# A residual kept in SBUF ahead of sliding window attention, and the sink's logit as a column of its scores

## The chip, the cores and the metric

The kernel runs on one core of a Trainium2 chip. A core has five engines that run side by side, each through its own list of instructions in order: TensorE (PE, matrix products), VectorE (DVE), ScalarE (ACT), GpSimd (POOL) and SyncE (SP), which here only issues DMA transfers. They wait for each other by semaphores. The metric is the time of one execution on the device in microseconds; several executions are taken, and their median is given.

## What is computed

Two transformer blocks follow each other on 1024 tokens with 1024 channels. The first has differential attention, stick-breaking attention, cross attention and an MLP, and ends in an RMS norm whose result is the second block's input `x`. The second block norms `x`, projects it by `w_in`, and runs three mixers: sliding window attention (8 heads, 2 key heads, window 128, with a sink per head), RWKV7 and a gated linear attention (GLA). Their outputs are joined, projected by `w_out`, normed and added to `x`. Two places matter here:

```python
# sliding window attention: a sink's logit is one more column of the softmax, and is dropped
s = jnp.where(valid[None, :, None, None], s, -jnp.inf)
sink = jnp.broadcast_to(sinks..., s.shape[:-1] + (1,))
p = jax.nn.softmax(jnp.concatenate([s, sink], axis=-1), axis=-1)[..., :-1]
o = jnp.einsum('bnhgqk,bnkhd->bnqhgd', p, vb)
...
# end of the second block
y = jnp.concatenate([attn, rwkv, gla], axis=-1) @ w_out
return x + gate[:, None] * _rmsnorm(y, g_post)
```

## The kernel before, in words

Activations lie with channels on the 128 partitions and tokens along the free axis. The 1024 tokens are worked in two halves of 512, the "first half" and the "second half". Products in 32 bits are made of three matmuls (lines 208 to 210) of a high and a low part; a weight tile is split into the two by ScalarE (line 200, `L200`) and then VectorE or GpSimd (`L201`). Streams between stages go through memory: `hd` is the first block's stream ahead of its last norm, `pd` the projections, `yd` the mixers' outputs, `zd` the first half's product with `w_out`, `out` the result.

The order of each engine's instructions is set by a scheduler that replays the program as it is written; what is written is itself an interleaving. `weave(main, fill, ratio)` takes steps of `main` and puts in between steps of `fill` of a cost in the given ratio; both are Python generators. In the part at hand there are two weaves:

- the first half's window attention (`g_window0`) with projections of the second half (`g_p2a`, `g_p2b`), at 0.9;
- as `main`, the second half's recurrences (`g_rec(1)`) and then its window attention (`g_tail`, that is `g_window(1)`); as `fill` (named `rest`), what is left of the projections, then `g_wout2` and `g_wout2a`, the product of the first half's mixers with `w_out`, at 0.28. Beside `g_wout2a` runs `g_final0`, the first half's last norm and sum. What of `rest` is left is used up inside `finish`, the second half's product with `w_out`, norm and sum.

`win_load` loads queries and keys of a half through three staging tiles named `ws` with the tag `wp`, and splits them (`stack_k`, `stack_q`; lines 441, 442, 454 to 457). `w_units` makes eight units of it, one per block of 128 queries and key head, each for four query heads, in three steps. Step `a`: scores (L1667, L1668) into PSUM; VectorE scales them, adds the mask's bias and writes them to `p` (L1670, twice per unit, two heads each) and takes the maximum (L1671, twice); then the sink: maximum with the sink's logit (L1673), sink less maximum (L1674), minus the maximum (L1675), its exponential on ScalarE (L1676). ScalarE takes the exponential of the four heads with their sums (L1678), VectorE adds the sink's share (L1681) and takes the reciprocal (L1682), ScalarE scales two heads (L1684) and GpSimd two (L1685). Step `tr`: transposes on TensorE (L1699), copied to SBUF by ScalarE (L1702). Step `pv`: product with the values (L1709), times the gate on VectorE (L1711), and for the second half a split into `yw`. `p` has the tag `wp` too, three buffers for the staging tiles and for the units' scores.

`g_final0` works through eight rows of 128 channels: it loads a row `h` of `hd` and a row `z` of `zd` (tiles `t` with the tag `t2`, five buffers, which others use too), makes `h` times gain and norm (L2314) and `z` times gate, gain and norm (L2316) on VectorE, adds them on GpSimd (L2317) and stores the row to `out`. `finish` loads weights (`wload`, L2332), splits them into `wb` and `wh`, loads the second half's residual `fh`, and multiplies `yw` with `wb` and `wh`.

## Time and profile of the kernel before

| what | us |
|---|---|
| median of 3 runs (2345.37 to 2354.68) | 2347.19 |
| the profiled execution | 2346.06 |
| its span, from its first instruction to its last | 2344.3 |
| TensorE busy in it (share of the span) | 2245.4 (96%) |
| VectorE busy | 1292.4 (55%) |
| ScalarE busy | 1034.7 (44%) |
| GpSimd busy | 691.2 (29%) |

The profile is a recording of one execution. It has a page with shares of each engine, and views of the trace behind it: a table by stretches of the span, the instructions of an engine in order of time with the idle time before each and what ended it (the timeline), groups of instructions by line and operation, what an engine waited for (the waits), and the chain of work that ended last, followed back from the last instruction. `L1675` is line 1675 of the kernel. Times of instructions are in microseconds from the span's start.

The first half's units run from about 1930 to 2005 us, the second half's from 2228 to 2300. The finish's first matmul starts at 2299.40 us, and the span ends 45 us later.

### The profile page before, as it was taken

Reading aid. Unit: us, or ns where it says so; the run is one execution under the profiler, and the core shown is the slowest. Engines: PE = TensorE matmul, PEld = TensorE weight load, DVE = VectorE, ACT = ScalarE, POOL = GpSimd, SP = SyncE. Lnnn points to the kernel's source line nnn. Section 1 sums busy time; section 2 is a strip of 40 time slices with the busy share of each in tenths; the row PEclk is TensorE's granted clock in tenths of the full one; section 3 lists DMA queues with packets and bytes.
Section 4 is the critical chain, followed back from the end, with each engine's and each line's share of the span. In section 5 each row is a group of like instructions: output and inputs, shape, how many; then the busy total and the mean of one; then the engine's idle time right before and its main releaser. Section 6 shows DMA issues by size and latency. Waiting matters only on the chain.

```text
span 2344.3 us, 34760 instructions
## 1 busy us (share of the span) xinstructions
PE 2245.4 (96%) x13056; PEld 1898.0 (81%) x13056; DVE 1292.4 (55%) x2312; ACT 1034.7 (44%) x2196; POOL 691.2 (29%) x1035
## 2 busy tenths in 40 slices
PE   8999999999999999999999999999999999989886
PEld 7898999988898888888888888887787776677765
DVE  7665656676754554422423422346846658656485
ACT  6655656674643424411311311344633348434463
POOL 4101100000500003556565650035322333224343
PEclk9999999999999999999999999999998999989898
DMA  4010010123241211222222221133343233533461
GB/s 135 28 42 23 31 39 28 46 77 124 66 140 54 99 37 45 75 79 72 77 83 72 78 74 45 52 124 122 119 134 105 74 127 100 166 126 105 131 208 50
DMA packets 116393, 200.06 MB, mean 85 GB/s; under 512 B 14048, under 2 KB 33792, under 8 KB 115456
## 3 DMA queue, kind: packets, MB, share of 16 engines
q1 hardware_dynamic: 111456, 184.72, 24.1%
q0 software_dynamic: 4768, 13.11, 1.7%
q8 instruction: 102, 1.67, 0.3%
q14 instruction: 67, 0.55, 0.1%
HBM read 163.70 MB, written 34.08 MB: 84 GB/s over the span
## 4 chain that ended last, share of the span: by engine, by line
PE 56%; DVE 8%; DMA 4%; ACT 2%; issue 2%; POOL 1%; SPq 0%; DVEq 0%; ACTq 0%; POOLq 0%
PE ps L208 17%; PE ps L209 16%; PE ps L210 16%; DVE act L1957 1%; DVE itmp L1954 1%; PE ps L1827 1%; PE ps L2124 1%; PE ps L1709 1%; DMA stg<-w2l 0%; PE ps L1785 0%; DVE wh L201 0%; DMA stg<-w2t 0%; PE ps L232 0%; DVE wp L1670 0%; ACT wh L200 0%
## 5 line engine op out<-in xcount | busy, mean ns | idle before, releaser
L208 PE MATMUL ps<-act,wh 128*128 128x512 f32 x1664 | 670.3, 405 | 7.5 <-ACT wh L200 5.7
L210 PE MATMUL ps<-act,wh 128*128 128x512 f32 x1664 | 658.1, 396 | 0.0
L209 PE MATMUL ps<-act,wh 128*128 128x512 f32 x1480 | 584.1, 395 | 2.6 <-DVE act L204 1.6
L200 ACT ACTIVATE wh<-stg 128x512 fp32r<-128x512 f32 x374 | 234.6, 630 | 581.4 <-PE ps L209 463.6
L208 PEld LDWEIGHTS ps<-act,wh 128*128 128x128 f32 x1664 | 318.9, 192 | 79.6 <-issue 6.1
L210 PEld LDWEIGHTS ps<-act,wh 128*128 128x128 f32 x1664 | 318.1, 191 | 68.7 <-issue 0.2
L209 PEld LDWEIGHTS ps<-act,wh 128*128 128x128 f32 x1480 | 282.1, 191 | 60.3 <-DVE act L204 2.4
L201 DVE TENSOR_TENSOR wh<-stg,wh 128x512 fp32r<-128x512 f32 x260 | 198.8, 767 | 154.4 <-ACT wh L200 152.9
L201 POOL TENSOR_TENSOR wh<-stg,wh 128x512 fp32r<-128x512 f32 x114 | 161.4, 1420 | 336.3 <-ACT wh L200 301.6
L907 DVE TENSOR_TENSOR act<-ps,act 128x512 f32<-128x512 f32 x112 | 77.0, 689 | 178.0 <-PE ps L210 177.8
L546 DVE TENSOR_TENSOR_SCAN pw<-pw,zero 128x128 f32<-128x128 f32 (+7 forms) x64 | 86.8, 1358 | 82.9 <-POOL pw L542 78.1
L247 POOL TENSOR_TENSOR nacc<-nacc,t 128x512 f32<-128x512 f32 x28 | 39.0, 1396 | 260.4 <-ACT t L246 256.0
L944 POOL TENSOR_TENSOR ad<-ad,cb 128x256 f32<-128x256 f32 x96 | 72.3, 754 | 146.6 <-DMA ad<-adaT 143.6
L1144 DVE SCALAR_TENSOR_TENSOR t<-ps,Rm 128x512 f32<-128x512 f32 x64 | 44.0, 691 | 127.6 <-PE ps L210 126.9
L949 POOL TENSOR_TENSOR ad<-ad 128x128 f32<-128x128 f32 (+5 forms) x288 | 97.3, 338 | 16.8
L208 PE MATMUL ps<-hid,wh 128*128 128x512 f32 x256 | 101.2, 395 | 0.0
L210 PE MATMUL ps<-hid,wh 128*128 128x512 f32 x256 | 101.1, 395 | 0.0
L209 PE MATMUL ps<-hid,wh 128*128 128x512 f32 x256 | 101.0, 395 | 0.0
L1145 ACT ACTIVATE t<-t 128x512 f32<-128x512 f32 x64 | 40.4, 631 | 135.8 <-DVE t L1144 135.8
L208 PE MATMUL ps<-wh,act 128*128 128x256 f32 x320 | 95.9, 300 | 0.0
L210 PE MATMUL ps<-wh,act 128*128 128x256 f32 x320 | 91.3, 285 | 0.0
L209 PE MATMUL ps<-wh,act 128*128 128x256 f32 x320 | 91.1, 285 | 0.0
(515 smaller groups left out, 4663.8 us busy)
## 6 DMA issues: line engine op xcount, KB each, us to landing
stg<-w2f SPq DMA_DIRECT2D x84, 256.0 KB, 3.1
stg<-w_dn SPq DMA_DIRECT2D x80, 256.0 KB, 2.8
stg<-w_up SPq DMA_DIRECT2D x64, 256.0 KB, 2.8
ad<-adaT POOLq DMA_DIRECT2D x96, 128.0 KB, 2.6
stg<-w2o SPq DMA_DIRECT2D x32, 256.0 KB, 2.7
pd<-t SPq DMA_DIRECT2D x30, 256.0 KB, 2.3
t<-yd SPq DMA_DIRECT2D x26, 256.0 KB, 3.5
rkd<-RK SPq DMA_DIRECT2D x4, 1280.0 KB, 5.7
```

The costliest lines, as they stand in the source:

```text
L200: nc.scalar.activation(hi, src, AF.Copy)
L201: (eng or nc.vector).tensor_tensor(lo, src, hi.bitcast(F32), ALU.subtract)
L208: mm(out, lh, rh, start=first, stop=False)
L209: mm(out, lh, rl, start=False, stop=False)
L210: mm(out, ll, rh, start=False, stop=last)
L247: nc.gpsimd.tensor_tensor(acc, acc, t[:, :n], ALU.add)
L546: V.tensor_tensor_scan(m[:, :w][:, ::-1], m[:, :w][:, ::-1], s.zero.to_broadcast([P, w]), 1.0, ALU.mult, ALU.add)
L907: s.nc.vector.tensor_tensor(hh, ps, hh, ALU.add)
L944: tt(t, t, cb[:, 256 * y : 256 * y + 256], ALU.mult)
L949: tt(acc[:, n, z, :] if w == 2 else a, a, b, ALU.add)
L1144: V.scalar_tensor_tensor(t, ps, 0.0, R[:, c * CH : (c + 1) * CH], ALU.max, ALU.mult)
L1145: nc.scalar.activation(t, t, AF.Square)
```

## The change

1. The residual of the first half, the eight rows of `hd`, is loaded whole into a tile `h0` in a pool of its own (`hp`), opened with the second window's pool, and the loads stand at the start of `g_final0`. The sum is written to `h0` and stored from there. Rows of `zd` are loaded one ahead. What is left of `rest` is used up before `finish`, and `hp` is closed; so the pool of `finish` (`fp`, with the tiles `wb`) takes its memory.
2. The sink's logit is written by GpSimd as a column of `p` next to the scores (257 columns). One maximum over four heads of 257 columns replaces two maxima and the line with the sink; ScalarE negates it; the exponentials and their sums take in that column. The lines 1673, 1674, 1675, 1676 and 1681 go.

```diff
@@ the weaves
-                tp = ExitStack()
+                tp, hp = ExitStack(), ExitStack()
                 def tail():
-                    yield from s.g_tail(tp.enter_context(tc.tile_pool(name="tp", bufs=1, reuse_waits="tile")))
+                    t = tp.enter_context(tc.tile_pool(name="tp", bufs=1, reuse_waits="tile"))
+                    h = hp.enter_context(tc.tile_pool(name="hp", bufs=1, reuse_waits="tile"))
+                    s.h0 = h.tile([P, KT, CH], F32, name="h0")
+                    yield from s.g_tail(t)
                 main = chain(s.g_rec(1), tail())
                 rest = chain(rest, s.g_wout2(b2), s.g_wout2a(s.g_final0(b2, out)))
                 weave(main, rest, 0.28, False)
+                for _ in rest:
+                    pass
+                hp.close()
                 with tp, tc.tile_pool(name="fp", bufs=1, reuse_waits="tile") as fp:
                     s.finish(fp, wp, out, rest)
@@ win_load
-        st = [mx.tile([P, 2, CH], F32, tag="wp", name=s.nm("ws"), bufs=3) for _ in range(3)]
-        t = [st[i // 2][:, i % 2, :] for i in range(6)]
+        st = [mx.tile([P, 4, 2 * P + 1], F32, tag="wp", name=s.nm("ws"), bufs=3) for _ in range(3)]
+        st = [x.rearrange("p a w -> p (a w)") for x in st]
+        t = [st[i // 2][:, i % 2 * CH : i % 2 * CH + CH] for i in range(6)]
@@ w_units
-                p = u["p"] = wn.tile([P, 4, 2 * P], F32, tag="wp", name=s.nm("wp"), bufs=3)
+                p = u["p"] = wn.tile([P, 4, 2 * P + 1], F32, tag="wp", name=s.nm("wp"), bufs=3)
                 t = s.sm.tile([P, 6, 4], F32, tag="wt", name=s.nm("wt"))
+                nc.gpsimd.tensor_copy(p[:, :, w : w + 1], sink[:, 4 * g : 4 * g + 4, None])
...
-                    V.tensor_reduce(t[:, 0, 2 * z : 2 * z + 2], pz, AX.X, ALU.max)
-                sk = sink[:, 4 * g : 4 * g + 4]
-                V.tensor_tensor(t[:, 1, :], t[:, 0, :], sk, ALU.max)
-                V.tensor_tensor(t[:, 2, :], sk, t[:, 1, :], ALU.subtract)
-                V.tensor_scalar(t[:, 1, :], t[:, 1, :], -1.0, None, ALU.mult)
-                nc.scalar.activation(t[:, 2, :], t[:, 2, :], AF.Exp)
+                V.tensor_reduce(t[:, 0, :], p[:, :, : w + 1], AX.X, ALU.max)
+                nc.scalar.activation(t[:, 1, :], t[:, 0, :], AF.Copy, scale=-1.0)
                 for h in range(4):
                     nc.scalar.activation(
-                        p[:, h, :w], p[:, h, :w], AF.Exp, bias=t[:, 1, h : h + 1], accum_out=t[:, 3, h : h + 1]
+                        p[:, h, : w + 1], p[:, h, : w + 1], AF.Exp, bias=t[:, 1, h : h + 1],
+                        accum_out=t[:, 3, h : h + 1],
                     )
-                V.tensor_tensor(t[:, 3, :], t[:, 3, :], t[:, 2, :], ALU.add)
                 V.reciprocal(t[:, 4, :], t[:, 3, :])
@@ g_final0
+        for mt in range(KT):
+            s.get_rows(s.h0[:, mt, :], s.hd, mt, 0)
...
+        zs = []
+        def zload(mt):
+            if mt < KT:
+                zs.append(s.tl(s.wk, [P, CH], "t2"))
+                s.get_rows(zs[mt], s.zd, mt, 0)
+        zload(0)
         for mt in range(KT):
-            h, z = s.tl(s.wk, [P, CH], "t2"), s.tl(s.wk, [P, CH], "t2")
-            s.get_rows(h, s.hd, mt, 0)
-            s.get_rows(z, s.zd, mt, 0)
+            h, z = s.h0[:, mt, :], zs[mt]
+            zload(mt + 1)
             V.scalar_tensor_tensor(h, h, s.gv[:, 4, mt : mt + 1], RF, ALU.mult, ALU.mult)
             yield
             V.scalar_tensor_tensor(z, z, s.GP[:, mt : mt + 1], RZ, ALU.mult, ALU.mult)
-            nc.gpsimd.tensor_tensor(z, z, h, ALU.add)
-            s.put_rows(out, mt, 0, z)
+            nc.gpsimd.tensor_tensor(h, z, h, ALU.add)
+            s.put_rows(out, mt, 0, h)
             yield
```

How this moves instructions is seen best in the order of the engines, second half's window. Line numbers of the changed kernel are higher: its scores' mask is L1679, the maximum L1680, the reciprocal L1687, GpSimd's scaling L1690; in `g_final0` the lines 2314, 2316 and 2317 are now 2328, 2330 and 2331. Numbers in names tell buffers apart: `wp_3724` and `wt_3725` are unit 1's scores and its small values, `wp_3739` unit 2's.

VectorE around unit 1, before:

```order
L1670 SCALAR_TENSOR_TENSOR wp_3724_20825<-ps_3726_20827,act_3363_18780 128x512
L2314 SCALAR_TENSOR_TENSOR t2_3744_20937<-t2_3744_20937,gv_74,rst_15471 128x512
L1670 SCALAR_TENSOR_TENSOR wp_3724_20825<-ps_3727_20834,act_3363_18780 128x512
L1671 TENSOR_REDUCE wt_3725_20826<-wp_3724_20825 128x2
L2314 SCALAR_TENSOR_TENSOR t2_3751_20969<-t2_3751_20969,gv_74,rst_15471 128x512
L1671 TENSOR_REDUCE wt_3725_20826<-wp_3724_20825 128x2
L1681 TENSOR_TENSOR wt_3710_20744<-wt_3710_20744 128x4
L1673 TENSOR_TENSOR wt_3725_20826<-wt_3725_20826,sink_20534 128x4
L1682 RECIPROCAL wt_3710_20744<-wt_3710_20744 128x4
L1674 TENSOR_TENSOR wt_3725_20826<-sink_20534,wt_3725_20826 128x4
L1675 TENSOR_SCALAR wt_3725_20826<-wt_3725_20826 128x4
```

and in the changed kernel, to the first rows of `z`:

```order
L1679 SCALAR_TENSOR_TENSOR wp_3724_20801<-ps_3726_20804,act_3363_18748 128x2x256
L1687 RECIPROCAL wt_3710_20716<-wt_3710_20716 128x4
L1679 SCALAR_TENSOR_TENSOR wp_3724_20801<-ps_3727_20810,act_3363_18748 128x2x256
L2328 SCALAR_TENSOR_TENSOR h0_20502<-h0_20502,gv_74,rst_15471 128x512 x8
L1680 TENSOR_REDUCE wt_3725_20802<-wp_3724_20801 128x4
L1679 SCALAR_TENSOR_TENSOR wp_3739_20871<-ps_3741_20874,act_3363_18748 128x2x256
L1679 SCALAR_TENSOR_TENSOR wp_3739_20871<-ps_3742_20880,act_3363_18748 128x2x256
L1680 TENSOR_REDUCE wt_3740_20872<-wp_3739_20871 128x4
L1687 RECIPROCAL wt_3725_20802<-wt_3725_20802 128x4
L2330 SCALAR_TENSOR_TENSOR t2_3744_20905<-t2_3744_20905,GP_13998,zacc_19972 128x512
L2330 SCALAR_TENSOR_TENSOR t2_3745_20907<-t2_3745_20907,GP_13998,zacc_19972 128x512
L2330 SCALAR_TENSOR_TENSOR t2_3751_20937<-t2_3751_20937,GP_13998,zacc_19972 128x512
```

The rows of `h` that lay one by one among the units now stand in one run of eight ahead of unit 1's maximum, the rows of `z` (a fourth follows) in a run behind unit 1's reciprocal.

GpSimd from unit 1's scaling on, before:

```order
L1685 TENSOR_TENSOR wp_3724_20825<-wp_3724_20825,wt_3725_20826 128x512
L2317 TENSOR_TENSOR t2_3745_20938<-t2_3745_20938,t2_3744_20937 128x512
L2317 TENSOR_TENSOR t2_3752_20970<-t2_3752_20970,t2_3751_20969 128x512
L201 TENSOR_TENSOR wh_3781_21133<-stg_3779_21130,wh_3780_21132 128x512
L1685 TENSOR_TENSOR wp_3739_20899<-wp_3739_20899,wt_3740_20900 128x512
L2317 TENSOR_TENSOR t2_3764_21039<-t2_3764_21039,t2_3763_21038 128x512
```

and in the changed kernel:

```order
L1690 TENSOR_TENSOR wp_3724_20801<-wp_3724_20801,wt_3725_20802 128x2x256
L201 TENSOR_TENSOR wh_3773_21061<-stg_3771_21058,wh_3772_21060 128x512
L2331 TENSOR_TENSOR h0_20502<-t2_3744_20905,h0_20502 128x512
L2331 TENSOR_TENSOR h0_20502<-t2_3745_20907,h0_20502 128x512
L2331 TENSOR_TENSOR h0_20502<-t2_3751_20937,h0_20502 128x512
L2331 TENSOR_TENSOR h0_20502<-t2_3762_21000,h0_20502 128x512
L1690 TENSOR_TENSOR wp_3739_20871<-wp_3739_20871,wt_3740_20872 128x2x256
L201 TENSOR_TENSOR wh_3778_21087<-stg_3776_21084,wh_3777_21086 128x512
L1671 COPY wp_3767_21029<-sink_20506 128x4
```

Four sums of rows now stand in a run ahead of unit 2's scaling, where two stood, and a copy of the sink into unit 4's scores follows.

ScalarE around unit 5's exponential, before (`wp_3769` is unit 4, `wp_3786` unit 5; `wh` and `wb` are weights, `act` with `ps` on the right a copy of transposed scores at L1702 and the eviction of a product at L2292):

```order
L1678 ACTIVATE wp_3769_21069,wt_3770_21070<-wp_3769_21069,wt_3770_21070 128x256 x4
L1702 ACTIVATE act_3363_18780<-ps_3784_21147 128x512
L1702 ACTIVATE act_3363_18780<-ps_3785_21153 128x512
L200 ACTIVATE wh_3858_21538<-stg_3857_21536 128x512
L2292 ACTIVATE act_3715_20790<-ps_3792_21203 128x512
L1684 ACTIVATE wp_3769_21069<-wp_3769_21069,wt_3770_21070 128x256 x2
L1676 ACTIVATE wt_3787_21160<-wt_3787_21160 128x4
L1678 ACTIVATE wp_3786_21159,wt_3787_21160<-wp_3786_21159,wt_3787_21160 128x256 x4
```

and in the changed kernel (`wp_3767` is unit 4, `wp_3783` unit 5):

```order
L1683 ACTIVATE wp_3767_21029,wt_3768_21030<-wp_3767_21029,wt_3768_21030 128x257 x4
L2297 ACTIVATE act_3715_20758<-ps_3779_21090 128x512
L1689 ACTIVATE wp_3767_21029<-wp_3767_21029,wt_3768_21030 128x256 x2
L1707 ACTIVATE act_3363_18748<-ps_3781_21101 128x512
L1707 ACTIVATE act_3363_18748<-ps_3782_21107 128x512
L200 ACTIVATE wb_3815_21316<-stg_3814_21314 128x512
L200 ACTIVATE wb_3818_21322<-stg_3817_21320 128x512
L200 ACTIVATE wb_3821_21328<-stg_3820_21326 128x512
L2297 ACTIVATE act_3715_20758<-ps_3788_21151 128x512
L1681 ACTIVATE wt_3784_21114<-wt_3784_21114 128x4
L1683 ACTIVATE wp_3783_21113,wt_3784_21114<-wp_3783_21113,wt_3784_21114 128x257 x4
```

The splits of the finish's weights, which stood among units 1 to 5, now begin right ahead of unit 5's exponential; the first of them waits for the stores of all rows of `h0`, whose memory it takes. The fourth `wb` and four `wh` follow among units 5 to 7.

## Rows read from the trace of the kernel before

**Rows 1.** The page's first line.
```profile
span 2344.3 us, 34760 instructions
```
**Rows 2.** Stretch table: stretch, length, busy us (instructions) per engine, PEclk, DMA share, GB/s.
```profile
2260.00:2302.00 42.00, 31.12 (x143) 20.16 (x140) 34.88 (x62) 25.55 (x73) 12.89 (x10) 0.96 0.50 163
```
**Rows 3.** TensorE's waits, 1915 to 2012 us: line, releaser: total us, times, longest.
```profile
PE ps L1699 <- ACT wp L1684: 4.6, 2, 2.4
PE ps L1709 <- ACT act L1702: 2.9, 2, 2.6
```
**Rows 4.** TensorE's waits, 2200 to 2302 us.
```profile
PE ps L1709 <- ACT act L1702: 8.5, 6, 3.7
PE ps L1699 <- ACT wp L1684: 3.8, 3, 1.6
PE ps L208 <- ACT ya L200: 2.7, 1, 2.7
```
**Rows 5.** Groups by line, 1920 to 2300 us: busy us, mean ns, idle us before.
```profile
L2317 POOL TENSOR_TENSOR t<-t,t 128x512 f32<-128x512 f32 x8 | 11.6, 1450 | 12.7 <-DVE t L2316 6.2 <-DVE wt L1673 5.1 <-DVE wt L1674 1.4
...
L1675 DVE TENSOR_SCALAR wt<-wt 128x4 f32<-128x4 f32 x16 | 10.9, 681 | 0.3
...
L1673 DVE TENSOR_TENSOR wt<-wt,sink 128x4 f32<-128x4 f32 x16 | 7.8, 488 | 0.0
...
L1681 DVE TENSOR_TENSOR wt<-wt 128x4 f32<-128x4 f32 x16 | 6.7, 418 | 8.7 <-ACT wp L1678 8.7
...
L2316 DVE SCALAR_TENSOR_TENSOR t<-t,GP,zacc 128x512 f32<-128x512 f32 x8 | 6.6, 835 | 0.0
...
L2314 DVE SCALAR_TENSOR_TENSOR t<-t,gv,rst 128x512 f32<-128x512 f32 x8 | 6.4, 797 | 1.3 <-DMA t<-hd 1.3
...
L1674 DVE TENSOR_TENSOR wt<-sink,wt 128x4 f32<-128x4 f32 x16 | 5.6, 349 | 0.2
```
**Rows 6.** Timeline of VectorE, second half's units: start us, us, line, operation.
```profile
2247.05 1.42 DVE L2316 SCALAR_TENSOR_TENSOR t<-t,GP,zacc 128x512 f32<-128x512 f32 x2
...
2266.80 1.52 DVE L2316 SCALAR_TENSOR_TENSOR t<-t,GP,zacc 128x512 f32<-128x512 f32 x1
...
2268.43 1.29 DVE L1675 TENSOR_SCALAR wt<-wt 128x4 f32<-128x4 f32 x1
```
**Rows 7.** Timeline of GpSimd, ahead of the first half's units and among the second's.
```profile
1911.89 2.90 POOL L218 TENSOR_TENSOR gr<-rsq,mhalf 128x16 f32<-128x16 f32 x1 [0.27 <-DVE lora L1451]
...
2232.36 1.02 POOL L218 TENSOR_TENSOR rz<-rsq,mhalf 128x4 f32<-128x4 f32 x1 [3.67 <-DVE rsq L217]
...
2268.40 1.29 POOL L2317 TENSOR_TENSOR t<-t,t 128x512 f32<-128x512 f32 x1 [0.63 <-DVE wt L1674]
```
**Rows 8.** Timeline of VectorE, ahead of the first half's units.
```profile
1913.57 5.99 DVE L442 TENSOR_TENSOR act<-ws,act 64x512 fp32r<-64x512 f32 x7
```
**Rows 9.** Timeline of TensorE: unit 3's values, and the finish's first matmul.
```profile
2272.43 1.98 PE L1709 MATMUL ps<-act,vt 128*128 128x512 f32 x4 [0.70 <-ACT act L1702]
...
2299.40 0.36 PE L208 MATMUL ps<-yw,wb 128*128 128x256 f32 x1
```
**Rows 10.** Chain that ended last, 2225 to 2345 us: start us, us, what.
```profile
2269.72 2.58 DMA out<-t
2272.32 3.98 DMA t<-hd
...
2292.56 2.06 ACT wp L1678 x8
```
**Rows 11.** Timeline of ScalarE from unit 5's exponential to its scaling.
```profile
2278.41 0.51 ACT L1678 ACTIVATE wp<-wp,wt 128x256 f32<-128x256 f32 x1 [2.06 <-DVE wt L1675]
...
2280.39 0.61 ACT L200 ACTIVATE yw<-t 128x512 fp32r<-128x512 f32 x1
2280.91 1.05 ACT L1702 ACTIVATE act<-ps 128x512 f32<-128x512 f32 x2
...
2282.47 0.91 ACT L1684 ACTIVATE wp<-wp,wt 128x256 f32<-128x256 f32 x2 [0.51 <-DVE wt L1682]
```

## The prediction

> **What bounds the kernel now.** The profiled execution took 2346.06 us, of which the span is 2344.3 us [rows 1]; 1.8 us lie around it. The sum below is made against 2346.06 us and then laid on the median of the three runs, 2347.19 us, 1.1 us above it. The change touches two stretches, the sliding attention of the first half (about 1920 to 2012 us) and of the second half with the first half's last norm woven into it (about 2226 to 2302 us). So I read four things in this order: how busy each engine is in the second stretch, what TensorE waits for in both, what the attention's small VectorE operations cost, and in what order the last units run. Elsewhere instructions keep their order but for small shifts, and I put that at zero.
>
> In 2260 to 2302 us TensorE works 31.1 of 42 us and VectorE 34.9 [rows 2]: VectorE is the busiest engine exactly where TensorE stops being full. TensorE's waits there name ScalarE: it waits for the transposed scores' copies (L1702), for the scaled scores (L1684) and once for ya, 8.5, 3.8 and 2.7 us [rows 4]; in the first window the same two lines make 4.6 and 2.9 us [rows 3]. ScalarE is only the last link. A unit is a chain: scores (TensorE), mask and maximum (VectorE), exponential (ScalarE), sum and reciprocal (VectorE), scaling (ScalarE and GpSimd), transposes, copies, values. Ceilings of a gain are therefore 7.5 us in the first window and 12.3 us in the second (the ya wait ends before the first unit's scores and is not touched).
>
> Inside the chain the four 128x4 lines L1673, L1674, L1675 and L1681 take 7.8 + 5.6 + 10.9 + 6.7 = 31.0 us in 64 instructions [rows 5], 1.94 us per unit, for four numbers per partition. They are stretched: one L1675 takes 1.29 us at 2268.43 [rows 6], and GpSimd's sum of a row starts at 2268.40 and takes 1.29 us [rows 7]. So what is removed is dear because it meets GpSimd.
>
> **The change part by part.** (1) Sink as column. Removed: the 64 VectorE instructions and the 16 exponentials L1676. Two maxima of half a unit become one of the whole, with four elements more: taken at zero. One column more in the exponentials: zero. Added on ScalarE: a negation of 128x4, which takes L1676's place. So each unit's chain loses 1.94 us less the negation.
>
> In the first window TensorE's 7.5 us are four waits [rows 3], each behind one or two such chains. At 1.94 us each the four would lose 7.8 us, at most the 7.5; at the other end nothing, if VectorE's other work there (the second half's projections) is late next. I take 3 us: these waits are 1.9 us on average and another engine's turn follows each.
>
> Added on GpSimd: 16 copies of 128x4. No copy of this form is in the trace; between zero and the 1.02 us of the power on 128x4 [rows 7] I take the upper, which is the nearest in shape. They lie in GpSimd's idle time but for one: unit 0's copy writes memory of the staging tile and waits until VectorE has split the queries that lie in it (L442, a run from 1913.57 to 1919.56 [rows 8]); behind it on GpSimd now stand a weight split and the power of gr, which before ran from 1911.89 to 1914.79 [rows 7]. The hold is between nothing and 4.8 us on gr, about 2 by the place of that tile in the run, and ScalarE and TensorE wait for gr to norm GLA's output. I take 0.7 us on the end, near the lower bound, since TensorE has projections to run meanwhile. In the second window the same hold meets a weight split that is used some microseconds later: zero, up to 2 us if it is not.
>
> (2) The residual h0. Eight loads of the old stream move ahead of the attention, into memory of their own. They sit on SP ahead of a store of zd and the last w_out loads; SP does nothing there that TensorE waits for, no wait in rows 4 is for a load, so zero. The waits of L2314 for its load, 1.3 us [rows 5], go. As the order shows, VectorE now runs all eight L2328 in one piece between unit 1's scores and its maximum: 8 x 0.80 = 6.4 us, where before two stood there. Unit 1's exponential is thus some 2 to 4 us later. TensorE does not feel it: the w_out matmuls of the first half lie beside it, and of the waits only the 0.7 us of unit 3's values at 2272.43 [rows 9] and at most L1699's 3.8 [rows 4] come before it ends. Without them these values start 4.5 us earlier at best, at 2268.
>
> (3) Rows. Four L2330 run in a piece; GpSimd adds four rows in a piece ahead of unit 2's scaling, and that scaling is due only when TensorE is through its w_out matmuls: zero. The first rows start at 2247.05 [rows 6], where they wait for the norm's factor, as before. Four adds of 1.45 us [rows 5] end near 2253. The next row of zd can be loaded only behind the first stores on SP, so the sixth and the eighth hang on two round trips of a load 3.98 [rows 10], a row 0.84 [rows 5], an add 1.45 and a neighbour's add ahead of it, about 7.7 us each: last add near 2268.4, its store landed 2.58 us [rows 10] later at 2271.
>
> (4) Weights of the last step. They used to be split among units 1 to 5; now wb takes h0's memory. So on ScalarE the first wb split waits for the last store of h0, and unit 5's exponential stands behind it. With three splits of 0.61 [rows 11], an eviction and the negation, unit 5's exponential starts near 2273.5; before it started at 2278.41 [rows 11]. From there ScalarE sets the pace: exponentials 2.06 [rows 10], copies 1.05, scaling 0.91, a split of yw and one of a weight 0.61 each [rows 11], 5.2 us per unit. Before, units 5 to 7 came every 7.1 us (2278.41 and 2292.56 [rows 10, 11]). The last unit took 6.8 us to the finish's first matmul at 2299.40 [rows 9]; two weight splits come into it, so 8.0. Sum: 2273.5 + 2 x 5.2 + 8.0 = 2291.9, a gain of 7.5 us. Bounds: if the stores land four microseconds sooner, 11; if every wait went, 12.3; if ScalarE stands longer, nothing or a loss (rivals). What follows 2299.40 is unchanged; the residuals fh are loaded in one piece ahead of the last four weight loads, which ScalarE wants only after unit 6's exponential: zero, up to 3 us if the burst is slow.
>
> Sum: 3.0 + 7.5 - 0.7 = 9.8 us less: 2336.3 us for the profiled execution, 2337 us on the median's basis.
>
> **A rule that speaks against it.** The stretched rows above come in pairs, a VectorE operation and a GpSimd operation of the same length [rows 6, 7]. The Trainium skill says in "SBUF — State Buffer", section "Who interferes with whom", that VectorE and GpSimd share one pair of SBUF ports as an exclusive lock: a VectorE instruction with two SBUF inputs, or one in a two-port mode as a tensor_scalar can take, contends with a GpSimd instruction that reads SBUF, and whoever issues first blocks the other for the whole instruction, while a maximum along the row never contends. The trace agrees for L1675 with its 1.29 us. By that rule the new runs, eight L2328 and four L2330 with two inputs in SBUF each, are exposed too; by the rows' means the sum stands as above, by the rule at its hardest it would be that of the first rival.
>
> **Rivals.** *The lock moves to the rows.* L2314 and L2316 average 0.80 and 0.84 us [rows 5], and a single one takes 1.52, at 2266.80 [rows 6]. If each of the twelve in the runs takes 0.6 more, 7 us, the last store lands at 2278 and unit 5's exponential comes at 2280.5; by the paces above the finish starts at 2298.9, and of the gain 0.5 + 3.0 - 0.7 = 2.8 us are left: 2344 us. For: the runs are long, and GpSimd has splits and adds beside them. Against: before, sixteen such rows beside the same adds averaged only 0.8.
>
> *TensorE's waits go almost wholly.* 12.3 + 5 - 0.7 = 16.6 us: 2331 us. For: VectorE was the busiest engine [rows 2] and loses 1.94 us a unit; against: ScalarE's own work of 5.2 us per unit.
>
> *Slower: ScalarE stands at the first wb split.* The last three rows of zd each need the store before them, so three round trips instead of two: 2253 + 3 x 7.7 + 2.58 = 2278.7, with 0.6 us of lock on four rows 2281. Unit 5's exponential then comes at 2283.5, the finish at 2302, 2.5 us later than before; with nothing won in the first window and both GpSimd holds at 2.7 us it is 5 us slower: 2352 us. It decides from a landing of about 2278.5 on. For: an in-order engine has the whole attention behind a wait that is only for memory. Against: stores and loads of before took 2.6 and 4.0 us [rows 10] while DMA was half busy [rows 2].
>
> *The change is not felt*, because another link of each chain was as late, lies between the first and the third rival.
>
> **How the numbers follow.** Forecast 0.42, lock 0.24, almost wholly 0.20, slower 0.14. The forecast's own range is 2332 to 2342 us. Half a percent, 11.7 us, is about what a measurement here can tell: below 2335.5 lie the larger gain and a little over two fifths of the forecast, 0.38 together; above 2358.9 that part of the slow case in which the finish's weights come late as well, 0.06; the rest is 0.56. The range reaches from just past the larger gain to near the slow case: 2329 to 2350 us.
>
> **What would show it.** Right: no VectorE instruction of 128x4 but the reciprocal in the units; TensorE's waits of rows 4 down to about 5 us; the finish's first matmul near 2291; unit 5's exponential behind wb splits. Wrong: a long ScalarE wait for the stores of out ahead of wb; L2328 or L2330 above 1.2 us on average (the lock); a first window whose TensorE waits are still near 7 us, or the power of gr done after 1919; a finish that waits for its last weights.

## The result and the profile after

The changed kernel takes 2333.8 us in the median (six runs, 2329.77 to 2336.51), the kernel before, run beside it, 2350.62 us (six runs, 2345.37 to 2357.62). The ratio is 0.9927 with a 95% interval of 0.991 to 0.9943: 0.73% faster, which is more than the half percent that a measurement of this kernel can tell from no change. The profiled execution of the changed kernel took 2334.33 us, 11.7 us less than that of before [rows 1], at the same mean granted clock of 0.972; its page begins

```profile
span 2332.5 us, 34687 instructions
```

The prediction was 2337 us in a range of 2329 to 2350. The time lies in the range, 3 us below the forecast; but the outcome it held likeliest, less than half a percent either way (0.56), is not the one that came.

TensorE's waits in the first window, which were 7.5 us over two lines [rows 3], are (line, releaser: total us, times, longest)

```profile
PE ps L1714 <- ACT act L1707: 5.0, 2, 3.5
```

and in the second window, where they were 8.5, 3.8 and 2.7 us [rows 4],

```profile
PE ps L1714 <- ACT act L1707: 7.5, 5, 2.9
PE ps L208 <- ACT ya L200: 2.6, 1, 2.6
```

The wait for scaled scores is gone in both. What is left is the wait for the copies of transposed scores, L1707 (before L1702). The stretch that the prediction's step (4) is about runs from TensorE's restart at the matmuls of ya to the finish's first matmul [rows 9]. In the timeline of the changed kernel's TensorE these are

```profile
2224.80 0.51 PE L208 MATMUL ps<-ya,wh 128*128 128x512 f32 x1 [2.64 <-ACT ya L200]
...
2287.96 0.36 PE L208 MATMUL ps<-yw,wb 128*128 128x256 f32 x1
```

that is 63.16 us; before they lay at 2229.73 and 2299.40, 69.67 us apart. So 6.5 us were won in the second window, and the restart itself came 4.93 us earlier. Of these 1.6 us were there before the first window began: both kernels run TensorE's instructions in the same order up to 1835 us, and at 1500 us the changed one is already 2.1 us ahead, a difference between the two executions. The first window, cut at the same two TensorE instructions in both kernels, as a row of the table by stretches (length; busy us of PE, PEld, which is TensorE's loading of weights, DVE, ACT, POOL; granted clock, DMA share, GB/s), first of the kernel before, then of the changed one:

```profile
1915.08:2004.56 89.48, 81.97 (x371) 59.79 (x370) 69.17 (x147) 63.55 (x156) 33.49 (x26) 0.96 0.40 133
```

```profile
1913.50:1998.83 85.33, 80.20 (x371) 58.66 (x370) 63.72 (x107) 63.02 (x155) 34.15 (x33) 0.98 0.41 136
```

It is 4.2 us shorter. TensorE's idle time in it (length less busy) fell from 7.5 to 5.1 us; the other 1.8 us are TensorE's own work, at a granted clock of 0.98 in place of 0.96. From there to the restart 0.8 us are given back. The same row for the stretch from the restart to the finish:

```profile
2229.73:2299.40 69.67, 57.17 (x273) 41.37 (x273) 59.36 (x108) 46.48 (x130) 27.58 (x21) 0.95 0.52 173
```

```profile
2224.80:2287.96 63.16, 55.62 (x273) 41.33 (x273) 51.58 (x66) 46.20 (x130) 28.70 (x26) 0.95 0.48 155
```

TensorE's idle time (length less busy) fell from 12.5 to 7.5 us with the same 273 matmuls and the same clock; VectorE lost 42 instructions and 7.8 us of work; ScalarE's work did not change. VectorE, busier than TensorE before (59.4 against 57.2 us), is less busy than it now (51.6 against 55.6).

The groups by line, 1920 to 2300 us (those of before are rows 5):

```profile
L1680 DVE TENSOR_REDUCE wt<-wp 128x4 f32<-128x1028 f32 x14 | 17.1, 1219 | 0.9 <-DVE wp L1679 0.5
...
L2330 DVE SCALAR_TENSOR_TENSOR t<-t,GP,zacc 128x512 f32<-128x512 f32 x8 | 11.3, 1446 | 1.2 <-DMA t<-zd 0.9 <-ACT zacc L236 0.3
L2328 DVE SCALAR_TENSOR_TENSOR h<-h,gv,rst 128x512 f32<-128x512 f32 x8 | 7.8, 1038 | 0.0
```

The four 128x4 lines with their 31.0 us are gone. The rows became dearer: L2330 takes 1446 ns where it took 835, L2328 1038 where it took 797 [rows 5], together 6.1 us of VectorE's busy time.

### The profile page after: what moved, and what is told of

It is laid out like the page before. It is cut to its first block, busy times and chain, and to the rows that moved or that the text cites. A ratio compares the mean times of both kernels' runs of the same rounds, so it can differ in the third digit from the quotient of the medians.

```text
span 2332.5 us, 34687 instructions
## 1 busy us (share of the span) xinstructions
PE 2240.5 (96%) x13056; PEld 1897.4 (81%) x13056; DVE 1276.4 (55%) x2232; ACT 1033.6 (44%) x2196; POOL 693.9 (30%) x1051
## 4 chain that ended last, share of the span: by engine, by line
PE 81%; DVE 8%; ACT 4%; DMA 3%; issue 2%; POOL 1%; SPq 0%; DVEq 0%; POOLq 0%; ACTq 0%
PE ps L208 22%; PE ps L209 21%; PE ps L210 21%; PE ps L561 3%; PE ps L482 2%; DVE itmp L1959 1%; PE ps L468 1%; PE ps L469 1%; DVE act L1962 1%; PE ps L699 1%; PE ps L1832 1%; PE ps L2129 1%; ACT wp L1683 1%; DMA pw<-xT 1%; PE ps L1714 1%
## 5 line engine op out<-in xcount | busy, mean ns | idle before, releaser
L949 POOL TENSOR_TENSOR ad<-ad 128x128 f32<-128x128 f32 (+5 forms) x288 | 98.4, 342 | 16.8
```

What stands on the lines that cost most here:

```text
L949: tt(acc[:, n, z, :] if w == 2 else a, a, b, ALU.add)
```

## The experiments

All runs are of one core. Each execution is listed with its mean granted TensorE clock, and that differs by itself (0.965 to 0.975), which moves the time by more than some of these edits do: over all kernels a thousandth of clock goes with 1.6 us. Beside median and ratio the table therefore has the mean laid to a clock of 0.971 by that common slope (uncertain by 0.6 to 0.9 us each, 0.3 for the kernel before), and, from each kernel's profile, the stretch of above with VectorE's work and TensorE's idle time in it and its clock. The experiments ran on three chips, in four sessions; the kernel before, run in each, lies at 2347.3 to 2348.9 us at that clock, so the chips differ by little more than these uncertainties.

| kernel | median us | ratio to before [95%] | at clock 0.971 | restart to finish | VectorE busy | TensorE idle | clock |
|---|---|---|---|---|---|---|---|
| before | 2350.3 (73 runs) | | 2348.2 | 69.67 | 59.4 | 12.5 | 0.95 |
| changed | 2333.8 | 0.9927 [0.991, 0.9943] | 2335.1 | 63.16 | 51.6 | 7.5 | 0.95 |
| e1_sink_only | 2333.71 | 0.9929 [0.9914, 0.9944] | 2337.0 | 64.74 | 48.9 | 8.7 | 0.95 |
| e2_h0_only | 2354.2 | 1.0006 [0.9993, 1.0019] | 2349.9 | 74.44 | 61.5 | 12.3 | 0.86 |
| e3_sink_first | 2343.54 | 0.9963 [0.9948, 0.9977] | 2343.3 | 71.67 | 58.6 | 12.9 | 0.93 |
| e11_sink_second | 2338.64 | 0.9958 [0.9944, 0.9972] | 2341.1 | 64.85 | 49.0 | 9.2 | 0.95 |
| e7_idle_ops | 2338.29 | 0.9944 [0.9928, 0.996] | 2339.9 | 67.86 | 56.6 | 10.0 | 0.92 |
| e6_before_adds_dve | 2351.56 | 1.0013 [0.9992, 1.0033] | 2347.9 | 72.97 | 56.4 | 13.8 | 0.91 |
| e5_adds_dve | 2336.06 | 0.9941 [0.9924, 0.9958] | 2338.6 | 65.01 | 53.6 | 7.9 | 0.92 |
| e4_h0_eight | 2338.32 | 0.9943 [0.9923, 0.9963] | 2336.7 | 63.67 | 52.4 | 6.7 | 0.92 |
| e9_wb_pool | 2338.83 | 0.9946 [0.9928, 0.9964] | 2337.0 | 62.61 | 52.4 | 7.5 | 0.95 |
| e10_scale_dve | 2341.6 | 0.9965 [0.9953, 0.9978] | 2339.4 | 69.46 | 55.1 | 9.8 | 0.85 |
| e12_rows_early | 2337.87 | 0.9944 [0.9925, 0.9964] | 2336.6 | 62.65 | 41.5 | 7.4 | 0.93 |

Where the clock of the stretch is under 0.95 its length is not compared; the idle time can be, with care.

**Which part of the change.** The column alone, and the residual alone:

```diff
 e1: the kernel before with the edits of win_load and w_units; g_final0 and the weaves as before
 e2: the kernel before with the edits of the weaves and g_final0; w_units as before
```

> Only the sink's column, in both windows; residual, rows and the order of the weaves as before. In the changed kernel's trace the second window's chain (restart of TensorE at the ya matmuls to the finish's first matmul) is 63.2 us long, 69.7 before, and the stretch ahead of it is 3.4 us shorter from 1890 us on. Theory (the small VectorE lines lengthened each unit's chain): the first window's 3.4 us come whole, the second window's chain shrinks by 3 to 5 of the 6.5 us, ratio 0.995 to 0.998. Rival, the rows moved ahead do the second window's work: its chain stays at 69 us or more. Rival, the column does all: chain near 63 us.

> Only the residual h0 with its pool, rows one ahead and the drained rest; the sink's four lines and its exponential as before. Theory: nothing in the first window; the second window's chain shrinks by 2 to 4 us, since the rows are through before unit 5, while the small lines meet GpSimd's sums more often in the dense stretch; ratio 0.997 to 1.0. Rival, the rows do it all: chain near 63 us, ratio 0.995 or less. Rival, h0 alone costs (ScalarE stands at the first weight split): ratio over 1.0.

The column gives 0.9929, the residual 1.0006, the whole 0.9927. The gain is the column's. At equal clock the whole is 1.9 us below the column alone, with an uncertainty of 1.2: what the residual adds to it is at most about 4 us and may be nothing. Alone it is 1.7 us above the kernel before, with an uncertainty of 0.7. Both expectations missed: the column alone was to give 0.995 to 0.998, and the 2 to 4 us that the residual was to take from the second window did not come (TensorE's idle time there is 12.3 us in place of 12.5).

**Which window.** The column in one window only, with the old code in the other:

```diff
+            def a_new():   # 257 columns, as in the changed kernel
+            def a_old():   # as before
...
+            a = a_new if c == 0 else a_old      # e3; e11 has c == 1
```

> The sink's column in the first half's window alone, all else as before. Theory: 2 to 4 us less than before, ratio 0.998 to 0.999, TensorE's waits in the first window 5 us in place of 7.5 and the rest of the 3.4 us from VectorE's freed time. Rival, the 3.4 us seen there are differences between executions: ratio 1.0 within its interval, and nothing between the projections' matmuls that is not there in the kernel before.

> The sink's column in the second half's window alone, residual and rows as before. Both windows' column was 0.9929 of the time before, the first window's alone 0.9963. Theory (the two windows' gains add up, each from its own chains): 0.9960 to 0.9975, the second window's chain 64 to 67 us in place of 69.7. Rival (the second window's gain needs the first one's, through a changed order or clock in between): 0.998 or more.

The first window gives 0.9963, the second 0.9958; their product 0.9921 is the change's 0.9927 within its interval, so the two gains add and neither is given back later. At equal clock the first is worth 4.9 us, the second 7.1; both are more than was expected. The waits of TensorE show the same crosswise. Of e3, 1910 to 2012 us, then 2190 to 2302 us:

```profile
PE ps L1743 <- ACT act L1736: 4.6, 2, 3.5
...
PE ps L1743 <- ACT act L1736: 8.5, 6, 3.7
PE ps L1733 <- ACT wp L1716: 4.2, 3, 2.2
```

and of e11, the same stretches:

```profile
PE ps L1733 <- ACT wp L1716: 6.2, 3, 3.5
PE ps L1743 <- ACT act L1736: 3.3, 3, 2.6
...
PE ps L1743 <- ACT act L1736: 7.2, 5, 2.9
PE ps L208 <- ACT ya L200: 4.4, 1, 4.4
PE ps L1674 <- DVE wp L1677: 0.9, 1, 0.9
PE ps L1733 <- ACT wp L1687: 0.5, 1, 0.5
PE ps L1733 <- POOL wp L1688: 0.5, 1, 0.5
```

The window that keeps the old code keeps its waits for scaled scores (4.2 us in e3's second, 6.2 in e11's first); the other loses all of them in e3, all but 1.0 us in e11 (0.5 behind ScalarE's half, 0.5 behind GpSimd's). The first window's length says the same: cut as above, it takes 89.0 to 90.3 us in the four profiles without the column there (before, e2, e6, e11), with TensorE idle for 7.4 to 9.5, and 82.5 to 86.7 in the seven with it and its other operations as in the changed kernel (changed, e1, e3, e4, e5, e9, e12), with TensorE idle for 4.2 to 5.4.

**VectorE's time, or the length of the result's chain?** The four small lines are put back into the changed kernel, written to a place that nobody reads, so that VectorE has their work again while the exponential does not wait for them. (This kernel does work that its result doesn't need.)

```diff
                 nc.scalar.activation(t[:, 1, :], t[:, 0, :], AF.Copy, scale=-1.0)
+                sk = sink[:, 4 * g : 4 * g + 4]
+                V.tensor_tensor(t[:, 5, :], t[:, 0, :], sk, ALU.max)
+                V.tensor_tensor(t[:, 5, :], sk, t[:, 5, :], ALU.subtract)
+                V.tensor_scalar(t[:, 5, :], t[:, 5, :], -1.0, None, ALU.mult)
...
+                V.tensor_tensor(t[:, 5, :], t[:, 3, :], t[:, 5, :], ALU.add)
                 V.reciprocal(t[:, 4, :], t[:, 3, :])
```

> The changed kernel with the four removed 128x4 operations put back on VectorE, their results used by nobody (the exponential waits for ScalarE's negation alone). Theory of the occupied engine and the lock: they take 1 us and more each beside GpSimd, stand in VectorE's order ahead of the next unit's mask and the reciprocal, and give back about half, 3 to 6 us against the changed kernel. Rival, only the chain of results counts: 0 to 2 us against the changed kernel.

In the groups by line of e7, 1920 to 2300 us, the four lines are

```profile
L1685 DVE TENSOR_SCALAR wt<-wt 128x4 f32<-128x4 f32 x16 | 6.4, 401 | 0.3
L1683 DVE TENSOR_TENSOR wt<-wt,sink 128x4 f32<-128x4 f32 x16 | 4.9, 304 | 0.1
L1684 DVE TENSOR_TENSOR wt<-sink,wt 128x4 f32<-128x4 f32 x16 | 4.6, 288 | 0.1
L1691 DVE TENSOR_TENSOR wt<-wt 128x4 f32<-128x4 f32 x16 | 3.7, 233 | 4.2 <-ACT wp L1687 4.2
```

19.6 us of VectorE's time, and the kernel is 4.8 us slower than the changed one at equal clock (uncertainty 1.2): about a third of the gain. TensorE's waits for scaled scores come back, with 1.3 us in the first window and 3.4 in the second; the first window, cut as above, takes 88.0 us, and TensorE idles 7.8 us of it. An operation whose result nobody needs still holds the next link behind it on an in-order engine. By difference the other two thirds belong to the shorter chain itself, to what the four cost more when they stand in it (31.0 us before), and to one maximum of 1.22 us in place of two of 0.67; these were not told apart.

**Does the price come from GpSimd's row sums?** The sums of rows (L2317, in the changed kernel L2331) are moved from GpSimd to VectorE, in the kernel before and in the changed one:

```diff
-            nc.gpsimd.tensor_tensor(z, z, h, ALU.add)      # e6; e5: (h, z, h)
+            V.tensor_tensor(z, z, h, ALU.add)
```

> The kernel before with the eight sums of rows (L2317) on VectorE. In the second window the four small lines took 17.4 of their 31.0 us. Theory of the lock: their stretched ones go with the sums, the four lines fall by 5 us or more in that window, and the time is 0 to 4 us below the kernel before although VectorE has 8 sums more. Rival (small operations are slow for another reason): the four lines stay near 17 us and the time rises by 2 to 5 us.

> The changed kernel with the eight sums of rows on VectorE in place of GpSimd. In the changed kernel a row of z takes 1.45 us in the mean beside these sums and 0.84 before. Theory of the lock: the row of z falls to 0.8 us or below, VectorE's added 8 x 0.7 = 5.6 us are paid by the 5 us of lock that go, rows are through sooner; the time within 2 us of the changed kernel. Rival (VectorE is the bound there and the stretching has another source): z rows stay above 1.2 us, and the time is 3 to 6 us above the changed kernel.

In e6 the four lines fall from 31.0 us [rows 5] to 22.2:

```profile
L1675 DVE TENSOR_SCALAR wt<-wt 128x4 f32<-128x4 f32 x16 | 7.2, 448 | 0.2
...
L1681 DVE TENSOR_TENSOR wt<-wt 128x4 f32<-128x4 f32 x16 | 6.4, 402 | 7.4 <-ACT wp L1678 7.4
...
L2317 DVE TENSOR_TENSOR t<-t,t 128x512 f32<-128x512 f32 x8 | 5.6, 700 | 0.0
L1673 DVE TENSOR_TENSOR wt<-wt,sink 128x4 f32<-128x4 f32 x16 | 4.3, 272 | 0.0
L1674 DVE TENSOR_TENSOR wt<-sink,wt 128x4 f32<-128x4 f32 x16 | 4.3, 268 | 0.2
```

So GpSimd's sums were behind about 9 of the 31 us, all of them in the second window (17.4 to 8.4 us), and the scaling of heads (L1685), which stays, is the next suspect for the rest; that was not tried apart. In e5 the rows L2330 fall from 1446 to 957 ns. Neither kernel got faster: 1.0013 against before, and e5 is 3.5 us above the changed kernel at equal clock. VectorE got 5.6 and 6.4 us of sums in exchange; that these take up what was freed is likely, but not shown.

**What holds the last units in the changed kernel?** Three edits, each aimed at one link of step (4): the residual as eight tiles, so that the first split of wb need not wait for the stores of all rows (e4); the high parts of the finish's weights made on GpSimd, which takes eight splits from ScalarE (e9); the scaling of two heads on VectorE in place of GpSimd (e10).

```diff
-                    s.h0 = h.tile([P, KT, CH], F32, name="h0")                                  # e4
+                    s.h0 = [h.tile([P, CH], F32, name=f"h0{i}") for i in range(KT)]
...
-            s.split(*wb[mt], st)                                                                # e9
+            G.tensor_copy(wb[mt][0], st)
+            V.tensor_tensor(wb[mt][1], st, wb[mt][0].bitcast(F32), ALU.subtract)
...
-                nc.gpsimd.tensor_tensor(p[:, 2:4, :w], ..., ALU.mult)                           # e10
+                for h in range(2, 4):
+                    V.tensor_scalar(p[:, h, :w], p[:, h, :w], t[:, 4, h : h + 1], None, ALU.mult)
```

> The changed kernel with h0 as eight tiles of a row each in place of one, so that a weight tile of the finish waits only for the stores of the rows whose memory it takes. In the changed kernel ScalarE stood 0.56 us for the last store ahead of the first weight split. Theory (that wait is off the path's weight): 0 to 1.5 us less than the changed kernel, ratio 0.992 to 0.993. Rival (ScalarE stands at the split and the whole attention behind it): 3 us or more less, ratio 0.991 or lower.

> The changed kernel with the high part of the finish's eight weight splits on GpSimd, which is nearly idle behind the last row's sum; ScalarE loses 8 x 0.52 = 4.2 us among units 4 to 7. Theory (ScalarE sets the pace there): 2 to 4 us below the changed kernel, the finish's first matmul about 60 us behind TensorE's restart at the ya matmuls in place of 63.2. Rival (the chain of a unit sets it, not ScalarE's sum): within 1 us. Rival (GpSimd's slower copies and the lock against VectorE's low parts): 1 to 4 us more.

> The changed kernel with the scaling of heads 2 and 3 on VectorE, one operation per head, in place of GpSimd's one of 1.04 to 1.49 us. Theory (what paces the last units is a unit's chain, of which GpSimd's scaling is a link of about 1.1 us beside ScalarE's 0.9): the chain from TensorE's restart at the ya matmuls to the finish's first matmul falls from 63.2 to 59 to 62 us, TensorE's waits in the first window from 5 to 3 or 4, 2 to 5 us below the changed kernel. Rival (VectorE is the bound, two more operations per unit): 0 to 4 us more.

e4 and e9 are not to be told from the changed kernel (1.6 and 1.9 us above it at equal clock, uncertainty 1.2 and 1.1). In e4's trace ScalarE no longer waits for the stores ahead of the first split, and nothing came of it. In e9 the stretch of above reads

```profile
2223.04:2285.65 62.61, 55.15 (x273) 41.27 (x273) 52.41 (x66) 42.45 (x122) 34.94 (x34) 0.95 0.49 157
```

ScalarE has 3.8 us less to do, and TensorE's idle time is the same 7.5 us. That does not show that ScalarE's work was off the path, since its trace has a wait that the changed kernel's has not. Unit 7's exponential starts 52.2 us behind the restart in place of 55.0. But GpSimd's copy of the fourth weight waits for the weight's load, VectorE's low part waits for that copy, the reciprocals of units 6 and 7 stand behind it on VectorE, and TensorE waits for their scaled scores:

```profile
2275.70 0.61 POOL L2351 CAST wb<-stg 128x512 fp32r<-128x512 f32 x1 [7.14 <-DMA stg<-w2o]
```

```profile
2276.34 1.14 DVE L2352 TENSOR_TENSOR wb<-stg,wb 128x512 fp32r<-128x512 f32 x1 [0.71 <-POOL wb L2351]
```

```profile
2278.29 2.14 PE L1704 MATMUL ps<-ident,wp 128*128 128x128 f32 x8 [4.25 <-ACT wp L1689]
```

What e9 would bring without that wait stays open. e10 is 4.3 us slower, and TensorE idles more in both windows (8.0 us in place of 5.1 in the first, 9.8 in place of 7.5 in the second); its group by line is

```profile
L1691 DVE TENSOR_SCALAR wp<-wp,wt 128x256 f32<-128x256 f32 x28 | 11.5, 453 | 0.2
```

about 0.9 us more on VectorE per unit, right between a unit's reciprocal and its transposes.

**Does any VectorE time count?** In the changed kernel eight rows L2328 stand in a run ahead of unit 1's maximum. e12 issues the loads of `h0`, the norm's factor and these rows ahead of the second window:

```diff
                     s.h0 = h.tile([P, KT, CH], F32, name="h0")
+                    RF = h.tile([P, CH], F32, name="RF0")
+                    for mt in range(KT):
+                        s.get_rows(s.h0[:, mt, :], s.hd, mt, 0)
+                    s.bcast(RF, s.rf[:, 0:4])
+                    for mt in range(KT):
+                        x = s.h0[:, mt, :]
+                        s.nc.vector.scalar_tensor_tensor(x, x, s.gv[:, 4, mt : mt + 1], RF, ALU.mult, ALU.mult)
                     yield from s.g_tail(t)
...
-            V.scalar_tensor_tensor(h, h, s.gv[:, 4, mt : mt + 1], RF, ALU.mult, ALU.mult)
```

> The changed kernel, with the loads of the first half's residual, the broadcast of its norm's factor and the eight h x gain x norm rows issued ahead of the last sliding attention's second window, into memory of their own; VectorE runs them in the idle time before TensorE's restart and no longer as one run of 7.76 us (eight rows, 1038 ns each in a row) between unit 1's scores and its maximum. Theory (every microsecond of VectorE in the units' stretch counts; 19.6 us of added VectorE work in the two windows cost 4 to 5 us): 1 to 3 us below the changed kernel, the chain from TensorE's restart to the finish 61 to 62.5 us in place of 63.2. Rival A (that run lay beside dense output matmuls and was hidden): within 1 us of the changed kernel, chain 63. Rival B (the rows stand ahead of the attention output's splits on VectorE and hold TensorE's restart): 1 to 4 us above it, the restart later by as much.

```profile
2223.17:2285.82 62.65, 55.24 (x264) 41.24 (x265) 41.51 (x60) 46.07 (x129) 27.76 (x26) 0.93 0.49 161
```

VectorE has 10 us less in the stretch, and TensorE idles 7.4 us as before; the time at equal clock is 2336.6 against 2335.1. By the numbers that is rival A, but the run was not simply hidden: TensorE's idle time lies elsewhere. Of the changed kernel's waits, 2.91 us lie among the matmuls of the first half's `w_out` (they are shown further down); in e12 none does, and behind the last of these matmuls, which starts at 2261.43, the waits make 7.4 us in place of 4.6. The longest is

```profile
2270.30 3.38 PE L1721 MATMUL ps<-act,vt 128*128 128x512 f32 x4 [3.68 <-ACT act L1714]
```

for copies that stand on ScalarE behind unit 5's exponential. That exponential's maximum was there at 2265.65 us; it started at 2267.69, behind weight splits of which two had waited 1.13 and 0.29 us for their loads. With e7 and e10 this says that VectorE's sum of work is not what counts: work put between the links of a unit cost 4 to 5 us in both, and work taken from ahead of unit 1's maximum moved TensorE's idle time from among the first half's `w_out` to behind it, and gave nothing.

No kernel of these beats the changed one.

## Why the prediction was right, and where it was not

**Mechanism.** That the small VectorE operations between maximum and exponential set TensorE's waits in both windows is shown by e1, e3 and e11: where the column stands in their place, the waits for scaled scores go. (The column also makes one maximum of two, 1.22 us in place of 2 x 0.67; 0.12 us a unit is too little for it.) That neither window's gain is given back later is shown by the product of the two gains.

**First window, 3.0 us.** Taken well under the ceiling of 7.5. The trace shows 2.4 us less wait, 4.2 us by the end of the window and 3.4 by the restart, the runs of e3 4.9 us at equal clock with an uncertainty of 0.9: somewhat small. The sum left out that TensorE's own work got 1.8 us shorter there, at a granted clock of 0.98 in place of 0.96.

**Second window, 7.5 us.** The trace shows 6.5, the runs of e11 7.1. Of the steps, the first half came out close: the last row's store was to land at 2271 and unit 5's exponential to start at 2273.5, in the times of before; laid to a restart 4.93 us earlier that is 2266.1 and 2268.6. The chain of waits and ScalarE's timeline of the changed kernel have

```profile
2261.91 1.28 POOL h L2331
2263.21 2.13 DMA out<-h
```

```profile
2265.45 1.67 ACT L200 ACTIVATE wb<-stg 128x512 fp32r<-128x512 f32 x3 [0.56 <-DMA out<-h]
...
2268.21 0.51 ACT L1683 ACTIVATE wp<-wp,wt 128x257 f32<-128x257 f32 x1
...
2274.53 0.21 ACT L1681 ACTIVATE wt<-wt 128x4 f32<-128x4 f32 x1 [1.44 <-DVE wt L1680]
2274.83 0.51 ACT L1683 ACTIVATE wp<-wp,wt 128x257 f32<-128x257 f32 x1
```

The store landed at 2265.34, ScalarE stood 0.56 us for it, and the exponential began at 2268.21. Part of this was luck, of two errors that cancel. The four adds were to end at 2253, which is 2248.1 here; they ended at 2250.85 (the GpSimd line further down), 2.8 us late. From there two round trips of 7.7 us each were to lead to the last add's end; it took 12.3 us, because the loads of the fifth to the seventh row left from 2248.41 on, beside the adds, and only the eighth had to wait for a later store.

**The step that failed is the one after it**: "from there ScalarE sets the pace, 5.2 us per unit". Unit 6's exponential came 6.6 us behind unit 5's, not 5.2, and ScalarE idled 1.44 us ahead of it for VectorE's maximum. (Unit 7's came 5.0 us behind unit 6's at 2279.80, and the finish 8.2 behind that: these two were as forecast.) VectorE had been at the mask, a split of wb, the mask again, a split of yw and the maximum:

```profile
2270.53 0.69 DVE L1679 SCALAR_TENSOR_TENSOR wp<-ps,act 128x512 f32<-128x512 f32 x1
2271.14 1.03 DVE L201 TENSOR_TENSOR wb<-stg,wb 128x512 fp32r<-128x512 f32 x1
2272.09 0.68 DVE L1679 SCALAR_TENSOR_TENSOR wp<-ps,act 128x512 f32<-128x512 f32 x1
2272.69 0.67 DVE L201 TENSOR_TENSOR yw<-t,yw 128x512 fp32r<-128x512 f32 x1
2273.29 1.21 DVE L1680 TENSOR_REDUCE wt<-wp 128x4 f32<-128x1028 f32 x1
```

From unit 5's exponential to the finish it took 19.75 us in place of 18.4, so the sum came out 1 us too large there. The prediction had moved the weights' splits to the last units and costed their ScalarE halves only; their VectorE halves stood in the chain. It also had TensorE's waits down to about 5 us: they are 10.3, because the copies' wait stayed, 2.91 us of it for a reason that is given under "The lock on the rows".

**GpSimd's hold, 0.7 us.** It did not occur. GpSimd's timeline ahead of the first window:

```profile
1907.78 0.19 POOL L1671 COPY wp<-sink 128x4 f32<-128x4 f32 x1 [3.04 <-DVE k L457]
...
1909.90 2.91 POOL L218 TENSOR_TENSOR gr<-rsq,mhalf 128x16 f32<-128x16 f32 x1 [0.32 <-DVE lora L1457]
1913.76 0.70 POOL L1671 COPY wp<-sink 128x4 f32<-128x4 f32 x1 [0.95 <-DVE act L442]
```

Unit 0's copy takes the staging tile that the keys lie in and waits for their split (L457), not for the queries'; the copies that wait for L442 stand behind gr. And a copy of 128x4 takes 0.19 to 0.70 us, not the 1.02 that was taken for it. The term was zero.

**The residual costs nothing.** Right within the noise (e2: 1.0006, and 1.7 us above before at equal clock with an uncertainty of 0.7). It also brings nothing alone, though L2314's 1.3 us of waits for loads go.

**The lock on the rows.** The sign that was named, L2330 above 1.2 us on average, did appear, with 1446 ns: 0.6 us more for each L2330, as that rival had it, and 0.24 for each L2328. Its consequence was not the one named. Four rows and four sums lie over each other:

```profile
2242.00 6.50 DVE L2330 SCALAR_TENSOR_TENSOR t<-t,GP,zacc 128x512 f32<-128x512 f32 x4 [0.26 <-ACT zacc L236]
```

```profile
2244.51 6.34 POOL L2331 TENSOR_TENSOR h<-t,h 128x512 f32<-128x512 f32 x4
```

The rival put the whole 7 us on the way to the last store; the store landed on time, in part by the luck told above, and the last row took only 0.76 us. But step (3) had put the two runs at zero, since TensorE has `w_out` matmuls meanwhile, and **that failed too**. These matmuls come to a stop at 2248.35. Unit 2's exponentials were through by 2245.8, but its reciprocal stood on VectorE behind the four rows, ScalarE's scaling behind the reciprocal, and the copies that TensorE needs next behind that scaling:

```profile
2249.62 0.16 DVE L1687 RECIPROCAL wt<-wt 128x4 f32<-128x4 f32 x1
```

```profile
2249.81 0.91 ACT L1689 ACTIVATE wp<-wp,wt 128x256 f32<-128x256 f32 x2 [2.97 <-DVE wt L1687]
```

```profile
2251.26 1.13 PE L1714 MATMUL ps<-act,vt 128*128 128x512 f32 x2 [2.91 <-ACT act L1707]
```

This is TensorE's longest wait in the window. At the 0.84 us of before the four rows would have been through some 3.2 us sooner. Whether the wait lengthened the span is not shown: in e12, where it is gone, the kernel is no faster. As to the rule cited (the Trainium skill, "SBUF — State Buffer", section "Who interferes with whom"), the trace agrees on both sides: the operations with two SBUF inputs stretch beside GpSimd's, and the maximum, which by it never contends, took at most 1.225 us in all 16 units.

**The total.** 9.8 us was the sum; the profiled execution is 11.7 us shorter, the runs at equal clock 13.1, the medians 16.8. Of the 1.9 us between sum and profile the hold that did not come makes 0.7 and the first window 0.4, the second window takes 1.0 away, and 1.6 lie ahead of the first window, where they are a difference between the executions and not the change's; the last 0.3 lie behind the finish's first matmul. Without these 1.6 the trace gives 10.1 us, near the sum, in which a hold that was not there and a second window taken too large nearly cancel. The runs' 13.1 has an uncertainty of 0.9; why it lies above the trace's 10.1 stays open. Of the 16.8 some 3 go with the executions' clock, 0.9718 on average in the six runs of the changed kernel and 0.9697 in all runs of before (0.0021 by 1.6 us a thousandth).

## What to carry to other kernels

A few numbers per partition can cost as much as a whole tile when they stand between two engines' turns: fold them into an operation that runs anyway (here a column of the scores), and look for them by the mean duration of tiny operations. Cost a moved step on every engine that it touches; here the ScalarE half of the weight splits was costed, and the VectorE half was in the chain. An engine's busy share tells that it may be the limit, not which of its work is: 10 us taken from VectorE ahead of unit 1's maximum moved TensorE's idle time and gave nothing at the end, 12 to 20 us put between the units' links of both windows cost 4 to 5. "TensorE has other matmuls meanwhile" holds only up to the next matmul in its order that needs the late result; look up where that one stands.

## What was not expected of the hardware

The executions' spread goes mostly with the granted clock. Over the 73 runs of the kernel before, time and mean granted clock correlate with −0.86: the three runs at 0.965 have a median of 2356.7 us, the four at 0.974 one of 2342.9. Which of the two drives the other the runs do not show; that a difference of medians of six runs can hold 3 us of it, they do.

A maximum over 1028 elements takes 1.22 us where two over 512 took 0.67 each: nearly nothing is won by joining them.
